# The 1/sqrt of the RMS norms as one power operation on GpSimd in place of seven VectorE operations

## The chip, the cores and the metric

The kernel runs on one core of a Trainium2 chip. The core has a matrix engine (TensorE, in the profile PE, with its weight loads as PEld), three engines for elementwise work (VectorE is DVE, ScalarE is ACT, GpSimd is POOL), and DMA queues that are issued mostly by SyncE (SP). The metric is the device time of one execution in microseconds; lower is better.

## The reference, cut to what matters

A stream of 256 prompt frames and another of 64 sample frames (320 tokens, 1024 features) goes through two layers: a Mamba-2 mixer with a ConvFFN, then, after a shared latent of that stream, multi-head latent attention (MLA) with a ConvFFN. All four sub-layers are wrapped in two norms, x = x + post_norm(f(pre_norm(x))), and the norm is

```
def rmsnorm(x, g):
    xf = x.astype(F32)
    y = xf * lax.rsqrt(jnp.mean(xf * xf, axis=-1, keepdims=True) + EPS)
    return (y * g.astype(F32)).astype(x.dtype)
```

The same function norms the gated output of the Mamba mixer in four groups of 512 features, the MLA latent (256 features) and the query latent (384). What the change touches is the `rsqrt` here and nothing else.

## The kernel before, in words

All activations lie transposed, features on the 128 partitions and the 320 tokens along the row, so that x is eight tiles of 128x320. Every projection is done with weights and activations split into a high and a low part, and three matmuls of a block (high x high, high x low, low x high: `mm3`, L281) stand for one. Weights come in by SP's queue into three buffers `wr`; ScalarE makes the high part `wh` (L326, L329), VectorE the low part `wl` (L328, L330); in MLA GpSimd makes some of the low parts, on the same line L328.

A norm sums over features, that is over partitions. It takes these steps: ScalarE squares the eight tiles and GpSimd or VectorE adds them up (L442); PE multiplies the sum with ones and so gets a column of sums per block of 128 tokens, 128x3 in PSUM (`toksum`, L362); VectorE turns it into the mean square plus epsilon (`mean`, L356, tile `nwv`; or L399, tile `nwl`, at a layer's end); `newton` (L336 to L351) makes 1/sqrt of it by an integer trick for the first guess and two steps of refinement, seven VectorE operations of 128x3, in lines L344 to L350; PE transposes the broadcast columns, which lays the result out over all partitions, 128x320 (`spread`, L369); and the result is used from PSUM or copied by ScalarE first (`rstd_sb`, L388).

There are 13 such norms: at the start of the Mamba input projection and of both up-projections (`outer`, which multiplies the un-normed x in the meantime and scales afterwards); one for each of the four gate groups of the Mamba mixer (`gate_steps`, applied on VectorE in L992); four at the ends of the sub-layers (`late_rstd`, tile `nwl`, where PE runs filler matmuls on a constant tile, L375, before and after the spread; none before the last one); a joint one of MLA with 128x6 columns (tile `rr`, L1110); and the one of the queries (tiles `vq` and `rq`, L1146 and L1147).

The kernel is written in program order, and a scheduler lays the instructions of each engine out anew from its own estimate of their durations. Only at the sub-layer boundaries is the order of VectorE and ScalarE kept as written (`region`). Each engine then runs its list strictly in order. `outer` records the end of the norm as `self.gate`, and the weight splits of the coming tiles are ordered behind that instruction.

Of the kernel before, what the change touches and what calls it, by code (L numbers as in the profile page):

```python
# [9 lines left out]
I32 = mybir.dt.int32  # L10
NOSYNC = mybir.DependencyInfo(mybir.DependencyClass.NoSync, mybir.DependencyReason.DATA)
AF = mybir.ActivationFunctionType
ALU = mybir.AluOpType
# [3 lines left out]
P = 128  # L17
# [32 lines left out]
RSU = 0.7235248917065753  # L50
RS = -0.6537252216689711, 0.8935148218557297, -3.0692990050469557, 2.7565293438350165
# [8 lines left out]
def _vec_layout():  # L60
    if VEC:
        return VEC
    o = 0
    for name, n in (
        ("mix_pre0", 8), ("mix_pre1", 8), ("mix_post0", 8), ("mix_post1", 8),
        ("ffn_pre0", 8), ("ffn_pre1", 8), ("ffn_post0", 8), ("ffn_post1", 8),
        ("kv_in", 8), ("kv_g", 2), ("q_g", 3),
        ("scw", 96), ("scb", 24), ("fcw0", 132), ("fcw1", 132), ("fcb0", 44), ("fcb1", 44),
        ("dtb", 1), ("alog", 1), ("sd", 16), ("sng", 16),
        ("sst", 72), ("fst0", 88), ("fst1", 88),  # L70
    ):
        VEC[name] = (o, n)
        o += n
    VEC["_n"] = (o, 0)
    return VEC
# [10 lines left out]
class Kern:  # L86
# [248 lines left out]

    def newton(self, v, pool, tag):  # L336

        nc = self.nc
        tt, ts, stt = nc.vector.tensor_tensor, nc.vector.tensor_scalar, nc.vector.scalar_tensor_tensor
        n = v.shape[1]  # L340
        r = self.t(pool, [P, n], tag, bufs=2)
        b = self.t(pool, [P, n], f"nwb{n}", bufs=2)
        u = self.t(pool, [P, n], f"nwu{n}", bufs=2)
        ts(r.bitcast(I32), v.bitcast(I32), -0.5, 1597463007.0, op0=ALU.mult, op1=ALU.add)  # L344
        tt(out=b, in0=r, in1=r, op=ALU.mult)
        stt(out=u, in0=b, scalar=RSU, in1=v, op0=ALU.mult, op1=ALU.mult)
        stt(out=b, in0=u, scalar=RS[0], in1=u, op0=ALU.add, op1=ALU.mult)
        stt(out=u, in0=u, scalar=RS[2], in1=u, op0=ALU.add, op1=ALU.mult)
        stt(out=r, in0=b, scalar=RS[1], in1=r, op0=ALU.add, op1=ALU.mult)
        self.nw_end = stt(out=r, in0=u, scalar=RS[3], in1=r, op0=ALU.add, op1=ALU.mult).ins  # L350
        return r  # L351

    def mean(self, src, dim, pool):
# [246 lines left out]
    def run(self):  # L600
        nc, tc, ctx, a = self.nc, self.tc, self.ctx, self.a
        _vec_layout()
        cp = ctx.enter_context(tc.tile_pool(name="cp", bufs=1, reuse_waits="tile"))
        self.wp = ctx.enter_context(tc.tile_pool(name="wp", bufs=1, reuse_waits="tile"))
        self.pst = None
        self.psum(**PSM)
        self.vec = self.t(cp, [P, VEC["_n"][0]], "vec")
        self.con = self.t(cp, [P, CON["cos"][0]], "con")
        self.x = self.t(cp, [P, KD, T], "x")
        self.ones = self.t(cp, [P, P], "ones")  # L610
        self.scratch = self.t(cp, [P, 1], "scratch")
        self.warm = self.t(cp, [P, 256], "warm", mybir.dt.bfloat16)
        self.pe_end = None
        nc.vector.memset(self.warm, 0.0)
        nc.vector.memset(self.ones, 1.0)
        nc.scalar.activation(out=self.scratch, in_=self.ones[:, 0:1], func=AF.Copy)
        self.busy(self.pb(), WARM)
        self.build_stream()
        self.wi = 0
        self.ident = self.c("ident")  # L620
        self.ssm()
        self.ffn(0)
        self.mla()
        self.ffn(1)
        self.residual(a["o_y"])
        self.yst.close()
        self.pst.close()
# [887 lines left out]
```

## Time and profile before

| what | value |
| --- | --- |
| median of 3 runs | 995.41 us (995.04, 995.41, 996.72) |
| the profiled execution | 998.17 us, span 996.4 us, mean granted clock 0.985 |
| PE busy | 959.9 us (96%) |
| VectorE busy | 757.7 us (76%), 1437 instructions |
| ScalarE busy | 605.1 us (61%) |
| GpSimd busy | 350.7 us (35%), 597 instructions |
| DMA | 135.55 MB, 136 GB/s on average |

Rows of the timeline have the start in us from the span's begin, the duration in us, the engine, the line, the operation, output<-inputs, the sizes and the count; in brackets stands how long the engine had been idle before, and what ended that. PE's weight loads (PEld) run ahead of its matmuls. The sub-layers end at about 272 (Mamba), 519 (first ConvFFN), 743 (MLA) and 983 us (second ConvFFN).

### The profile page before, as it was taken

The page shows a single profiled execution, that of the slowest core. Times are in us where ns is not written, and L with a number is a line of the kernel's source. Part 1 is how long each engine was busy: PE and PEld are TensorE (multiplying, and loading weights), DVE is VectorE, ACT ScalarE, POOL GpSimd, SP SyncE. Part 2 cuts the span into 40 slices and gives each one's busy share as a digit, 9 for nine tenths or more (in the row PEclk, how much of TensorE's full clock was granted, in tenths as well). Part 3 has the DMA queues.
Part 4 walks back from the last instruction along what each step waited for, and adds up shares of the span by engine and source line. Part 5 has one row for each costly group of instructions (what it writes and reads, how often), then busy time and mean ns, then how long its engine had stood idle before and what let it go on. Part 6 is the DMA issues. An engine that isn't in the chain of part 4 may idle for free.

```text
span 996.4 us, 18044 instructions
## 1 busy us (share of the span) xinstructions
PE 959.9 (96%) x6585; PEld 929.7 (93%) x6585; DVE 757.7 (76%) x1437; ACT 605.1 (61%) x1201; POOL 350.7 (35%) x597
## 2 busy tenths in 40 slices
PE   7899999999999999999999999999999999999995
PEld 6899999979989999999999899999999999999994
DVE  7879889797488998774547998886538999775433
ACT  6568886734556687664443677774544778665330
POOL 4823231200045665430005765530004767441001
PEclk9999999998999999999999999999999999999998
DMA  7376646442334544455641222133443455445531
GB/s 251 120 212 190 188 138 204 132 154 96 101 94 131 169 149 150 149 186 165 194 125 35 86 70 78 50 102 114 143 136 105 132 167 169 150 143 145 152 115 54
DMA packets 45802, 135.55 MB, mean 136 GB/s; under 512 B 5392, under 2 KB 9616, under 8 KB 45712
## 3 DMA queue, kind: packets, MB, share of 16 engines
q1 hardware_dynamic: 45424, 134.05, 43.1%
q8 instruction: 52, 0.85, 0.4%
q14 instruction: 38, 0.31, 0.1%
q10 hardware_dynamic: 288, 0.33, 0.1%
HBM read 130.25 MB, written 4.11 MB: 135 GB/s over the span
## 4 chain that ended last, share of the span: by engine, by line
PE 79%; DVE 10%; DMA 3%; POOL 3%; issue 3%; ACT 2%; SPq 0%; POOLq 0%; ACTq 0%; DVEq 0%
PE pm L283 46%; PE pm L284 23%; PE px L283 2%; DMA dc<-acd 2%; PE pr L362 1%; PE px L952 1%; DVE wl L328 1%; POOL xacc L442 1%; PE px L284 1%; PE px L943 1%; PE px L935 1%; ACT wh L326 1%; DVE mx L1267 1%; POOL xn L478 1%; DVE y L450 1%
## 5 line engine op out<-in xcount | busy, mean ns | idle before, releaser
L328 DVE TENSOR_TENSOR wl<-wr,wh 128x1024 fp32r<-128x1024 f32 (+2 forms) x204 | 244.8, 1201 | 115.4 <-ACT wh L326 114.6
L326 ACT ACTIVATE wh<-wr 128x1024 fp32r<-128x1024 f32 (+4 forms) x235 | 227.6, 972 | 154.2 <-PE pm L283 126.7
L283 PE MATMUL pm<-xnh,wh 128*128 128x320 f32 x784 | 243.4, 312 | 2.1 <-ACT xnh L329 1.8
L283 PE MATMUL pm<-xnl,wh 128*128 128x320 f32 x784 | 245.0, 313 | 0.3 <-DVE xnl L330 0.3
L284 PE MATMUL pm<-xnh,wl 128*128 128x320 f32 x784 | 243.1, 311 | 0.0
L283 PEld LDWEIGHTS pm<-xnh,wh 128*128 128x128 f32 x784 | 147.6, 189 | 4.8 <-ACT xnh L329 2.0
L283 PEld LDWEIGHTS pm<-xnl,wh 128*128 128x128 f32 x784 | 147.8, 189 | 1.7 <-issue 1.2
L284 PEld LDWEIGHTS pm<-xnh,wl 128*128 128x128 f32 x784 | 147.8, 189 | 1.2 <-issue 1.2
L284 PE MATMUL pm<-ah,wl 128*128 128x320 f32 x452 | 141.0, 313 | 0.0
L283 PE MATMUL pm<-al,wh 128*128 128x320 f32 x452 | 140.4, 311 | 0.0
L283 PE MATMUL pm<-ah,wh 128*128 128x320 f32 x452 | 139.9, 313 | 0.0
L649 DVE SCALAR_TENSOR_TENSOR cv<-ext,vec,cv 128x322 f32<-128x322 f32 x176 | 97.1, 566 | 5.4 <-ACT cv L647 3.0
L643 POOL COPY fsave<-ext 128x2 f32<-128x2 f32 x88 | 72.2, 821 | 53.4 <-ACT ext L640 49.1
L636 POOL MEMSET ext<- 128x2 f32 (+1 forms) x112 | 10.8, 98 | 221.3 <-DVE al L330 66.0
L283 PEld LDWEIGHTS pm<-ah,wh 128*128 128x128 f32 x452 | 85.3, 190 | 1.7 <-ACT ah L329 1.5
L284 PEld LDWEIGHTS pm<-ah,wl 128*128 128x128 f32 x452 | 85.4, 189 | 1.1 <-issue 1.0
L283 PEld LDWEIGHTS pm<-al,wh 128*128 128x128 f32 x452 | 85.5, 189 | 0.0
L328 POOL TENSOR_TENSOR wl<-wr,wh 128x512 fp32r<-128x512 f32 (+2 forms) x31 | 43.7, 1425 | 102.3 <-ACT wh L326 100.9
L283 PE MATMUL pm<-xgl,wh 128*128 128x320 f32 x220 | 68.4, 314 | 1.0 <-DVE xgl L426 1.0
L284 PE MATMUL pm<-xgh,wl 128*128 128x320 f32 x220 | 68.3, 314 | 1.0 <-DVE wl L330 0.7
L283 PE MATMUL pm<-xgh,wh 128*128 128x320 f32 x220 | 62.6, 316 | 4.6 <-ACT xnh L329 2.4
L647 ACT ACTIVATE cv<-ext,vec 128x322 f32<-128x322 f32 x88 | 57.0, 654 | 10.0 <-POOL ext L637 6.8
(396 smaller groups left out, 2138.5 us busy)
## 6 DMA issues: line engine op xcount, KB each, us to landing
wr<-w_up SPq DMA_DIRECT2D x76, 512.0 KB, 3.3
wr<-w_in SPq DMA_DIRECT2D x37, 512.0 KB, 3.8
wr<-w_dn SPq DMA_DIRECT2D x32, 512.0 KB, 3.5
wr<-w_out SPq DMA_DIRECT2D x16, 512.0 KB, 3.6
wr<-w_o SPq DMA_DIRECT2D x16, 512.0 KB, 3.4
wr<-w_up_k SPq DMA_DIRECT2D x16, 384.0 KB, 3.1
wr<-w_dn SPq DMA_DIRECT2D x16, 384.0 KB, 3.2
dc<-acd SPq DMA_DIRECT2D x8, 512.0 KB, 7.0
```

Of the source, the lines that this page charges most:

```text
L283: for i in (mm(out, wh, xh, start=first, stop=False), mm(out, wh, xl, start=False, stop=False), mm(out, wl, xh, start=False, stop=last)):
L284: mm(out, wl, xh, start=False, stop=last)):
L326: self.high_ins = nc.scalar.activation(out=hdst, in_=src, func=AF.Copy).ins
L328: return lambda: e.tensor_tensor(out=ldst, in0=src, in1=hdst.bitcast(F32), op=ALU.subtract)
L362: i = self.nc.tensor.matmul(ps[:, o + b:o + b + 1], acc[:, l0:l0 + 128], self.ones[:, 0:1], start=True, stop=True)
L442: nc.gpsimd.tensor_tensor(out=acc, in0=acc, in1=s, op=ALU.add)
L450: tt(out=yk, in0=yk, in1=r, op=ALU.mult)
L478: nc.gpsimd.tensor_tensor(out=xn, in0=self.x[:, k, :], in1=rstd, op=ALU.mult)
L636: nc.gpsimd.memset(ext[:, 0:m], 0.0)
L643: nc.gpsimd.tensor_copy(out=rows_out[:, 0, :], in_=ext[:, TP:TP + m])
L647: nc.scalar.activation(out=c, in_=ext[:, 0:n], func=AF.Identity, scale=w(0), bias=b)
L649: nc.vector.scalar_tensor_tensor(out=c, in0=ext[:, i:i + n], scalar=w(i), in1=c, op0=ALU.mult, op1=ALU.add)
```

## The change

`newton` becomes one GpSimd operation: the mean square raised to the power of a tile that holds -0.5. That tile, `half`, is 128x8 and set once at the start of the kernel by VectorE. `self.nw_end`, the instruction that `outer` passes on as `self.gate`, is now that GpSimd operation. The two scratch tiles `nwb` and `nwu` are gone. Whole:

```
--- before.py
+++ after.py
@@ -335,19 +335,8 @@
 
     def newton(self, v, pool, tag):
 
-        nc = self.nc
-        tt, ts, stt = nc.vector.tensor_tensor, nc.vector.tensor_scalar, nc.vector.scalar_tensor_tensor
-        n = v.shape[1]
-        r = self.t(pool, [P, n], tag, bufs=2)
-        b = self.t(pool, [P, n], f"nwb{n}", bufs=2)
-        u = self.t(pool, [P, n], f"nwu{n}", bufs=2)
-        ts(r.bitcast(I32), v.bitcast(I32), -0.5, 1597463007.0, op0=ALU.mult, op1=ALU.add)
-        tt(out=b, in0=r, in1=r, op=ALU.mult)
-        stt(out=u, in0=b, scalar=RSU, in1=v, op0=ALU.mult, op1=ALU.mult)
-        stt(out=b, in0=u, scalar=RS[0], in1=u, op0=ALU.add, op1=ALU.mult)
-        stt(out=u, in0=u, scalar=RS[2], in1=u, op0=ALU.add, op1=ALU.mult)
-        stt(out=r, in0=b, scalar=RS[1], in1=r, op0=ALU.add, op1=ALU.mult)
-        self.nw_end = stt(out=r, in0=u, scalar=RS[3], in1=r, op0=ALU.add, op1=ALU.mult).ins
+        r = self.t(pool, [P, v.shape[1]], tag, bufs=2)
+        self.nw_end = self.nc.gpsimd.tensor_tensor(out=r, in0=v, in1=self.half[:, 0:v.shape[1]], op=ALU.pow).ins
         return r
 
     def mean(self, src, dim, pool):
@@ -613,6 +602,8 @@
         self.pe_end = None
         nc.vector.memset(self.warm, 0.0)
         nc.vector.memset(self.ones, 1.0)
+        self.half = self.t(cp, [P, 8], "half")
+        nc.vector.memset(self.half, -0.5)
         nc.scalar.activation(out=self.scratch, in_=self.ones[:, 0:1], func=AF.Copy)
         self.busy(self.pb(), WARM)
         self.build_stream()
```

Over the whole kernel this takes 91 instructions (13 x 7) from VectorE's list, puts one memset there, and adds 13 to GpSimd's. Lines of the changed kernel are 11 lower than those of before from `mean` to `outer`, 9 lower behind the memset. Since the scheduler counts with other engines and durations, it also lays out the list of the other engines anew, most of all in the Mamba stage; the boundaries keep their order.

In the rows that follow, each engine's list stands in the order in which it runs; the numbers behind the names tell tiles apart and differ between the two programs.

First place: GpSimd at the boundary from the first ConvFFN to MLA. `fsave` is the saved end of the convolution, `wl` a low part of MLA's first weights. Before:

```order
L644 COPY fsave_3201<-ext_5379 128x2
L328 TENSOR_TENSOR wl_6334<-wr_6118,wh_6333 128x768
L454 TENSOR_TENSOR x_72<-x_72,y_5408 128x320
L442 TENSOR_TENSOR xacc_6256<-xacc_6256,xsq_6269 128x320
L442 TENSOR_TENSOR xacc_6256<-xacc_6256,xsq_6276 128x320
```

With the change:

```order
L635 COPY fsave_3163<-ext_5325 128x2
L339 TENSOR_TENSOR rk_6176<-nwl_6159,half_78 128x3
L328 TENSOR_TENSOR wl_6272<-wr_6064,wh_6271 128x768
L443 TENSOR_TENSOR x_72<-x_72,y_5354 128x320
L431 TENSOR_TENSOR xacc_6194<-xacc_6194,xsq_6207 128x320
```

The power stands between the last copy and the weight split, so the split runs behind it.

Second place: VectorE in `outer` of the first up-projection, around 302 us. Before:

```order
L328 TENSOR_TENSOR wl_3442<-wr_3391,wh_3441 128x896
L356 TENSOR_SCALAR nwv_3469<-pr_3465 128x3
L344 TENSOR_SCALAR rk_3471<-nwv_3469 128x3
L345 TENSOR_TENSOR nwb_564_3472<-rk_3471 128x3
L346 SCALAR_TENSOR_TENSOR nwu_565_3473<-nwb_564_3472,nwv_3469 128x3
L347 SCALAR_TENSOR_TENSOR nwb_564_3472<-nwu_565_3473 128x3
L348 SCALAR_TENSOR_TENSOR nwu_565_3473<-nwu_565_3473 128x3
L349 SCALAR_TENSOR_TENSOR rk_3471<-nwb_564_3472,rk_3471 128x3
L350 SCALAR_TENSOR_TENSOR rk_3471<-nwu_565_3473,rk_3471 128x3
L330 SCALAR_TENSOR_TENSOR wl_3484<-wr_3415,vec_70,wh_3483 128x128
L328 TENSOR_TENSOR wl_3484<-wr_3415,wh_3483 128x896
```

With the change:

```order
L328 TENSOR_TENSOR wl_3396<-wr_3345,wh_3395 128x896
L345 TENSOR_SCALAR nwv_3423<-pr_3419 128x3
L330 SCALAR_TENSOR_TENSOR wl_3430<-wr_3369,vec_70,wh_3429 128x128
L328 TENSOR_TENSOR wl_3430<-wr_3369,wh_3429 128x896
L330 SCALAR_TENSOR_TENSOR wl_3462<-wr_3393,vec_70,wh_3461 128x128
```

The weight splits, which read two tiles of SBUF, follow the mean at once.

Third place: PE around a gate norm late in the Mamba stage, at about 219 us before (`rk` in the transposes of line 369, now 358; `ah` and `al` are the gated activations of earlier groups, lines 918 to 952 the scan). Before:

```order
L362 MATMUL pr_2357<-ones_73,sz_2135 128x1 x3
L935 MATMUL px_2535<-dc_359_2125,xa_2531 64x128 x8
L943 MATMUL px_2544<-ct_1847,hp_2475 128x128 x4
L952 MATMUL px_2551<-xa_2532,bcs_2428 128x512
L918 MATMUL px_2603<-con_71,xs_1911 64x128
L918 MATMUL px_2603<-con_71,xs_1971 64x128
L918 MATMUL px_2603<-con_71,xs_2029 64x128
L918 MATMUL px_2603<-con_71,xs_2089 64x128
L369 MATMUL pr_2373<-con_71,rk_2363 128x128 x3
L935 MATMUL px_2612<-dc_361_2130,xa_2608 64x64 x8
L943 MATMUL px_2621<-ct_1847,h_387_2318 128x64 x4
L952 MATMUL px_2658<-xa_2609,bcs_2490 128x512
```

With the change:

```order
L284 MATMUL pm_2539<-ah_103,wl_2467 128x320
L283 MATMUL pm_2540<-ah_103,wh_2466 128x320
L283 MATMUL pm_2540<-al_104,wh_2466 128x320
L358 MATMUL pr_2343<-con_71,rk_2341 128x128 x3
L284 MATMUL pm_2540<-ah_103,wl_2467 128x320
L283 MATMUL pm_2541<-ah_103,wh_2466 128x320
L283 MATMUL pm_2541<-al_104,wh_2466 128x320
L284 MATMUL pm_2541<-ah_103,wl_2467 128x320
```

Where the transposes of the norm stood between steps of the scan with no other matmul near, they stand among the matmuls of the output projection; the steps of the scan are spread over that stretch in the same way.

## The prediction

> **What bounds the kernel now.** I read the head of the page first, then the chain that ended last, then the busy time by stretches of the span.
>
> ```profile
> span 996.4 us, 18044 instructions
> PE 959.9 (96%) x6585; PEld 929.7 (93%) x6585; DVE 757.7 (76%) x1437; ACT 605.1 (61%) x1201; POOL 350.7 (35%) x597
> PE 79%; DVE 10%; DMA 3%; POOL 3%; issue 3%; ACT 2%; SPq 0%; POOLq 0%; ACTq 0%; DVEq 0%
> ```
>
> TensorE is busy for 959.9 of 996.4 us, so at most about 36 us is to be had without touching the matmuls. VectorE, from which the change takes work, holds only 10% of the last chain. Two stretches of the Mamba stage (columns: stretch, length, then busy us of PE, PEld, DVE, ACT and POOL, granted clock, DMA share, GB/s) show where VectorE is the fuller engine:
>
> ```profile
> 18.00:50.00 32.00, 26.87 (x169) 26.05 (x170) 28.27 (x66) 16.78 (x28) 23.00 (x27) 0.95 0.36 117
> 200.00:240.00 40.00, 37.64 (x257) 33.20 (x257) 35.67 (x72) 15.16 (x25) 0.24 (x2) 0.91 0.36 123
> ```
>
> In the first, PE is idle for 32.00 - 26.87 = 5.1 us and VectorE for 3.7; in the second PE is idle for 2.4 us and its clock is down to 0.91. So seven small VectorE operations can matter in two ways: as latency, where everything waits for one norm (the layer boundaries), and as room on VectorE (the Mamba stage). The first can be counted from the trace, the second only bounded.
>
> **The price of the power operation, d.** No instruction of this trace raises to a power, so d is unknown and everything is worked out as a function of it. The nearest rows are two-input operations on GpSimd (columns: least/median/largest ns):
>
> ```profile
> L442 POOL TENSOR_TENSOR xacc<-xacc,xsq x28: 877/1008/1629, 7.7 to 763.2; 128x320 f32<-128x320 f32 x28
> L328 POOL TENSOR_TENSOR wl<-wr,wh x31: 1007/1295/2083, 520.7 to 652.6; 128x512 fp32r<-128x512 f32 x15, 128x768 fp32r<-128x768 f32 x8, 128x384 fp32r<-128x384 f32 x8
> ```
>
> The least of 320 columns is 877 ns, and the least of the other row, which I take for its 384 columns, 1007 ns: (1007 - 877)/64 = 2.0 ns a column and 877 - 320 x 2.03 = 227 ns fixed. Three columns of an ordinary operation would be 0.23 us: the lower bound. For the upper one, if a power takes as much work as the seven operations it stands for, it is 7 x 0.23 = 1.6 us. I take d = 0.8 us, between the two and nearer to the plain operation, since most of it is the fixed part. It may also be above 1.6 us: that is a rival below. Where a result crosses from one engine to the next I add 0.1 us each way (VectorE to PE took 985.50 - 985.39 = 0.11 in the rows that follow), so that the new path from the mean square to PE's transposes is 0.2 + d.
>
> The Trainium skill (GPSIMD Engine Reference, section 4.1, Engine selection) says that a two-input elementwise operation is about twice as slow on GpSimd as on VectorE, which speaks against such a move. This trace agrees for 320 columns: 877 ns on GpSimd, 0.49 us for the VectorE sum of line 452 below. By that rule alone, with VectorE's 0.16 us for a three-column operation, d would be an estimated 0.32 us, and the terms below would add up to about 0.5 us more at the end, 0.5 us more at the ConvFFN-to-MLA boundary and nothing elsewhere.
>
> **Boundary by boundary.** The last norm has nothing beside it:
>
> ```profile
> 983.98 0.16 DVE L399 SCALAR_TENSOR_TENSOR nwl<-pr,nwv 128x3 f32<-128x3 f32 x1 [3.94 <-PE pr L362]
> 985.23 0.16 DVE L350 SCALAR_TENSOR_TENSOR rk<-nwu,rk 128x3 f32<-128x3 f32 x1
> 985.50 0.30 PEld L369 LDWEIGHTS pr<-con,rk 128*128 128x128 f32 x3 [1.65 <-issue]
> ```
>
> The mean square is there at 984.14 and PE starts to spread at 985.50: 1.36 us. It becomes 0.2 + 0.8, so the gain is 1.16 - d = **0.36**, all of it on the path, since the output follows.
>
> The boundary from the first ConvFFN to MLA:
>
> ```profile
> 520.10 1.52 PEld L375 LDWEIGHTS <-warm 128*128 128x128 bf16 x14
> 520.39 0.16 DVE L399 SCALAR_TENSOR_TENSOR nwl<-pr,nwv 128x3 f32<-128x3 f32 x1 [2.94 <-PE pr L362]
> 520.70 1.80 POOL L328 TENSOR_TENSOR wl<-wr,wh 128x768 fp32r<-128x768 f32 x1 [77.44 <-ACT wh L326]
> 520.79 1.73 DVE L345 TENSOR_TENSOR nwb<-rk 128x3 f32<-128x3 f32 x1
> 523.49 0.30 PEld L369 LDWEIGHTS pr<-con,rk 128*128 128x128 f32 x3 [1.87 <-issue]
> 524.66 0.49 DVE L452 TENSOR_TENSOR xgh<-x,y 128x320 fp32r<-128x320 f32 x1
> ```
>
> Here one of the seven takes 1.73 instead of 0.16 us: it starts 0.09 us after GpSimd's 1.80 us split and ends 0.02 us after it. In the new order the power stands ahead of that split on GpSimd (first place of the section on the change). So it runs from 520.65 to 520.65 + d, PE can spread at 520.75 + d but not before its filler matmuls end at 520.10 + 1.52 = 521.62, and the split runs from 520.65 + d to 522.45 + d. VectorE's sum into xgh (line 452), for which the next stage waits, reads two SBUF tensors as line 345 did, and would be held until the split ends: 523.25 at d = 0.8 against 524.66, a gain of 2.21 - d = **1.41**. The cost has moved from one victim to the next, which is later.
>
> The boundary from MLA to its ConvFFN, and the one from the Mamba stage to the first ConvFFN:
>
> ```profile
> 744.11 1.52 PEld L375 LDWEIGHTS <-warm 128*128 128x128 bf16 x14
> 744.39 0.16 DVE L399 SCALAR_TENSOR_TENSOR nwl<-px,nwv 128x3 f32<-128x3 f32 x1 [3.06 <-PE px L362]
> 745.86 0.30 PEld L369 LDWEIGHTS px<-con,rk 128*128 128x128 f32 x3 [0.24 <-DVE rk L350]
> ```
>
> ```profile
> 273.23 2.46 PEld L375 LDWEIGHTS <-warm 128*128 128x128 bf16 x14
> 273.52 0.16 DVE L399 SCALAR_TENSOR_TENSOR nwl<-pr,nwv 128x3 f32<-128x3 f32 x1 [1.74 <-PE pr L362]
> 275.76 0.65 PEld L369 LDWEIGHTS pr<-con,rk 128*128 128x128 f32 x3
> ```
>
> At 744 the fillers end at 745.63 and the spread starts at 745.86: the gain is **0.23** as long as 744.55 + 0.2 + d is below 745.63 (d up to 0.88), and 1.11 - d after that. At 273 the fillers run to 275.69 and set the start: **0** for d up to 275.76 - 273.88 = 1.9, since the norm is covered today already.
>
> **Inside the stages.** The norms at the start of a projection (`outer`) and the joint one of MLA (six columns) have matmuls beside them:
>
> ```profile
> 302.77 0.16 DVE L356 TENSOR_SCALAR nwv<-pr 128x3 f32<-128x3 f32 x1 [5.22 <-PE pr L362]
> 304.12 0.35 DVE L330 SCALAR_TENSOR_TENSOR wl<-wr,vec,wh 128x128 fp32r<-128x128 f32 x1
> 304.39 1.08 DVE L328 TENSOR_TENSOR wl<-wr,wh 128x896 fp32r<-128x896 f32 x1
> 305.18 0.39 PEld L369 LDWEIGHTS pr<-con,rk 128*128 128x128 f32 x3
> ```
>
> ```profile
> 19.30 0.16 DVE L356 TENSOR_SCALAR nwv<-pr 128x3 f32<-128x3 f32 x1 [0.25 <-PE pr L362]
> 21.67 0.30 PEld L369 LDWEIGHTS pr<-con,rk 128*128 128x128 f32 x3 [0.79 <-PE pm L284]
> ```
>
> ```profile
> 544.87 0.17 DVE L344 TENSOR_SCALAR rr<-vs 128x6 int32<-128x6 int32 x1
> 546.68 0.39 PEld L369 LDWEIGHTS pr<-con,rr 128*128 128x128 f32 x3
> ```
>
> PE spreads 305.18 - 302.93 = 2.25, 21.67 - 19.46 = 2.21 and 546.68 - 544.87 = 1.81 us after the mean, and in none of the three was the norm the last to arrive. So they count **0** while 0.2 + d stays below these, and the cover that would be gone is 2.0 us (1.6 for the six columns). The third such norm, of the last ConvFFN, is of the same form. The weight splits behind the norm move up on VectorE (second place of the section on the change), which nobody waited for.
>
> The norm of the queries:
>
> ```profile
> 556.22 0.15 DVE L1146 SCALAR_TENSOR_TENSOR vq<-pr,ex 128x3 f32<-128x3 f32 x1
> 557.47 4.15 POOL L1202 TENSOR_TENSOR qs<-q,qs 32x320 fp32r<-32x320 f32 x6 [1.00 <-ACT qs L1196]
> 560.81 0.15 DVE L1148 TENSOR_SCALAR sc<-rq 128x2 f32<-128x2 f32 x1
> ```
>
> ```profile
> PE pm L283 <- DVE qll L328: 1.1, 3, 0.6
> ```
>
> The seven stretch over most of 556.4 to 560.8, partly held by GpSimd's qs. GpSimd is idle for 1.00 us ahead of those, where the power fits for d up to about 1. PE's waits for qll there are 1.1 us in all: gain between 0 and 1.1, and I take half, **0.5**.
>
> **The Mamba stage.** Four gate norms run while VectorE is nearly full:
>
> ```profile
> 217.17 0.15 DVE L344 TENSOR_SCALAR rk<-nwv 128x3 int32<-128x3 int32 x1
> 219.51 0.16 DVE L350 SCALAR_TENSOR_TENSOR rk<-nwu,rk 128x3 f32<-128x3 f32 x1
> 221.97 1.47 DVE L992 TENSOR_TENSOR yg<-yg,pr 128x1280 f32<-128x1280 f32 x1
> ```
>
> The first six of the seven take until about 218.2 and the last waits behind two others. That is some 1.2 us of VectorE for each of five norms (four gates, one `outer`), 6 us in all. The scheduler has also laid the stage out anew: where the scan of the last group had no independent matmul between its steps, dense projection matmuls now stand between (third place of the section on the change), which can fill the 2.4 us of idle PE and the 9% of clock that are lost in 200 to 240 (0.09 x 40 = 3.6 us). Against that, an order that a planner made on its own idea of d can also bring new waits. Bounds: a gain of 2.4 + 3.6 = 6, and a loss of 3, about one such wait at two norms. I take **1.5**, the middle of the two.
>
> **Sum.** 0.36 + 1.41 + 0.23 + 0 + 0 + 0.5 + 1.5 = 4.0 us. The profiled execution took 998.17 us (1.8 around its span of 996.4), so it becomes 994.2. The runs have their median at 995.41, 2.76 below it; taking this off gives **991.4 us**. A measurement of this kernel tells about 0.2%, 2 us, from no change.
>
> **Rivals.** *B, no change that can be measured.* d lies between 1.1 and 1.6 us, or the Mamba stage gives nothing. At d = 1.3 with no gain there: 2.21 - 1.3 = 0.9, 1.11 - 1.3 = -0.2, 1.16 - 1.3 = -0.1, together 0.6 us: 994.8. For it: five of the thirteen norms are covered, and the bound of 1.6 is not far off. Against it: the 1.73 us stall goes in either case.
>
> *C, the power is slow.* It decides from d = 1.6 on, where the three exposed boundaries give 0.6 - 0.5 - 0.4, hence nothing. At d = 3: 273 costs 1.1 (3 - 1.9), 520 costs 0.8, 744 costs 1.9, the end costs 1.8, three outer norms 1.0 each, the query norm some 2, and the joint one, if six columns take twice as long, 6.2 - 1.8 = 4.4: 15.0 us, less the 1.5 of the Mamba stage: 13.5, or 1009. At d = 2, where the outer norms just hold: 0.1 - 0.2 + 0.9 + 0.8 + 0 + 1 + 2.4 = 5.0, less 1.5: 3.5, or 998.9. For it: all GpSimd rows here are sums, differences, products and copies, so nothing excludes it. Against it: it has only three or six columns, and 1.6 us is already seven times the plain operation.
>
> *D, VectorE keeps GpSimd from its operands.* What happened to VectorE at 520 happens the other way round in the Mamba stage:
>
> ```profile
> L643 POOL COPY ssave<-ext x24: 176/663/5697, 26.7 to 176.0; 128x3 f32<-128x3 f32 x24
> 27.64 5.70 POOL L643 COPY ssave<-ext 128x3 f32<-128x3 f32 x1
> 27.81 1.22 DVE L328 TENSOR_TENSOR wl<-wr,wh 128x1024 fp32r<-128x1024 f32 x1
> ```
>
> A copy of three columns that takes 176 ns by itself took 5.70 us while VectorE went from one operation with two SBUF inputs to the next; the median is 663 ns. The Trainium skill (SBUF — State Buffer, section Who interferes with whom) states this as a lock: a VectorE operation with two SBUF inputs and a GpSimd operation that reads SBUF shut each other out. The trace agrees with it in both directions. In the new order VectorE's splits follow the mean at once, so at 302 two pairs of them (0.35 + 1.08 each) could hold the power until 302.93 + 2.86 = 305.8 and PE until 306.7, 1.5 us later than today; the same at 19. If at each of four gates the wait lasts about as long as that copy's and 2 us of it is not covered, this is 3 + 8 against 2.5 for the boundaries and the queries: 8.5 us slower, 1003.9 with nothing from the new layout. It decides from about half a us at each gate on (3 + 2 against 2.5). Against it: it limits itself, since a VectorE that reaches the gate has to wait for the norm and so lets go.
>
> **How the numbers follow.** The forecast (d from 0.3 to 1.1, the new layout of the Mamba stage a small gain) gets 0.49, B 0.20, C 0.18 and D 0.13. The forecast's own range: at best d = 0.3, 0.86 + 1.87 + 0.23 (the spread at 520 cannot start before 521.62, 1.87 earlier), 1.1 for the queries and 4 for the Mamba stage, 8.1 us, 987.3; at worst d = 1.1, 1.2 and nothing more, 994.2. The whole range takes in the lower end and a bit of the 6 us bound, 986.5, and C up to d = 3, 1009. Faster by over 0.2%: 0.49; within: 0.21; slower: 0.30 (C and D).
>
> **What would show it.** Line 339 in the new profile gives d and its spread: 0.3 to 1.1 us for three columns and a largest value under 3 us. At the end, the nwl-to-spread distance falls from 1.36 to about 1.0 us. At 520 the 1.73 us row is gone, and GpSimd's split starts after the power. At 273, 302 and 545 the spread stands where it stood. In the last 40 us of the Mamba stage PE's idle time falls below 2.4 us and the clock rises above 0.91. The forecast is wrong if line 339 has a median above 1.6 us (then C), or if PE or VectorE waits for line 339 at the gates for more than 1 us each (then D).

## The result, and the profile after

The changed kernel takes 987.62 us (median of 6 runs, 985.95 to 989.06) beside 996.72 us for the kernel before (median of 6): ratio 0.9915, 95% interval 0.9899 to 0.9931, or 8.5 us faster; the two medians are 9.1 us apart. The forecast was 991.4 us with a range from 986.5 to 1009.0. The sign was right and the time lies in the range, but the gain is about twice the forecast 4.0 us. Which of its terms were wrong is the matter of what follows. One execution below, the profiled one of the kernel with the power operation in the Mamba stage alone, ran at a granted clock of 0.56 and took 1556.21 us; it enters no ratio, and no number below is from its trace.

The head of the page of the changed kernel:

```profile
span 985.2 us, 17961 instructions
PE 956.4 (97%) x6585; PEld 930.2 (94%) x6585; DVE 744.3 (76%) x1347; ACT 603.7 (61%) x1201; POOL 368.3 (37%) x610
PE 83%; DVE 10%; POOL 2%; issue 2%; ACT 1%; DMA 0%; POOLq 0%; DVEq 0%; ACTq 0%
```

VectorE lost 13.4 us of busy time, and its share of the last chain is 10% as before. PE's share rose from 79% to 83% of a shorter span.

The power operation has line 339 in the changed kernel (least/median/largest ns, then first and last start):

```profile
L339 POOL TENSOR_TENSOR rk<-nwv,half x7: 851/900/1764, 19.6 to 756.0; 128x3 f32<-128x3 f32 x7
L339 POOL TENSOR_TENSOR rk<-nwl,half x4: 848/848/850, 268.2 to 973.9; 128x3 f32<-128x3 f32 x4
L339 POOL TENSOR_TENSOR rr<-vs,half x1: 1332/1332/1332, 534.6 to 534.6; 128x6 f32<-128x6 f32 x1
L339 POOL TENSOR_TENSOR rq<-vq,half x1: 1090/1090/1090, 546.1 to 546.1; 128x3 f32<-128x3 f32 x1
```

At the four sub-layer ends d is 0.85 us for three columns. For the seven norms inside the stages the median is 0.90, and for the queries it is 1.09. The one row of six columns has 1.33, which gives an estimate of (1332 - 848)/3 = 161 ns a column and 365 ns fixed. The forecast took 0.8.

The two stretches of the Mamba stage in the changed kernel, in the columns of the table in the prediction:

```profile
18.00:50.00 32.00, 25.90 (x157) 24.73 (x156) 29.54 (x64) 16.95 (x28) 27.16 (x28) 0.89 0.35 117
200.00:240.00 40.00, 40.00 (x296) 36.99 (x296) 29.60 (x45) 17.57 (x23) 2.79 (x4) 1.00 0.40 132
```

From 200 to 240 us PE is full, at full clock, and does 296 matmuls where it did 257. From 18 to 50 it is a little worse off than before.

The time by stages, in two executions each of both kernels (the second profiles are two of the runs below). A stage runs from one norm's mean square on VectorE to the next, or to PE's spread:

| stage | before | before, again | after | after, again | gain |
| --- | --- | --- | --- | --- | --- |
| start to the first boundary's mean square | 273.52 | 273.15 | 267.92 | 268.18 | 5.3 |
| first boundary, to the mean square of `outer` | 29.25 | 27.50 | 27.66 | 27.80 | 0 to 1.6 |
| first ConvFFN, to the one after it | 213.99 | 213.97 | 212.37 | 212.37 | 1.6 |
| ConvFFN-to-MLA boundary, to the joint norm's spread | 26.29 | 26.30 | 24.75 | 24.75 | 1.5 |
| MLA, to its last mean square | 197.71 | 197.85 | 197.90 | 197.86 | 0 |
| MLA-to-ConvFFN boundary, to the mean square of `outer` | 21.73 | 21.71 | 21.54 | 21.54 | 0.2 |
| second ConvFFN | 217.86 | 217.86 | 217.85 | 217.85 | 0 |
| last mean square to the end | 12.42 | 12.44 | 11.59 | 11.72 | 0.8 |

Without the first boundary the gains add up to 9.4 us, and 6.9 of them lie where no norm is exposed: 5.3 us in the Mamba stage and 1.6 us in the first ConvFFN. The 1.6 us that the first boundary seems to have gained comes and goes in the kernel before itself: its first execution had its filler matmuls there at a lower clock (14 weight loads in 2.46 us), the second at full clock (1.52 us), and then its distance is 27.50. Whether the change makes the lower clock rarer there, two executions each can't say.

### The profile page after: what moved, and what is told of

Read it like the earlier page. It is cut to its first block, busy times and chain, and to the rows that moved or that the text cites. A ratio compares the mean times of both kernels' runs of the same rounds, so it can differ in the third digit from the quotient of the medians.

```text
span 985.2 us, 17961 instructions
## 1 busy us (share of the span) xinstructions
PE 956.4 (97%) x6585; PEld 930.2 (94%) x6585; DVE 744.3 (76%) x1347; ACT 603.7 (61%) x1201; POOL 368.3 (37%) x610
## 4 chain that ended last, share of the span: by engine, by line
PE 83%; DVE 10%; POOL 2%; issue 2%; ACT 1%; DMA 0%; POOLq 0%; DVEq 0%; ACTq 0%
PE pm L283 48%; PE pm L284 24%; PE px L283 2%; DVE wl L328 1%; PE px L943 1%; PE px L926 1%; PE px L284 1%; PE pr L351 1%; POOL xacc L431 1%; PE px L934 1%; DVE xnl L330 1%; DVE cv L640 1%; PE px L909 1%; DVE y L439 1%; DVE x L443 1%
## 5 line engine op out<-in xcount | busy, mean ns | idle before, releaser
L284 PE MATMUL pm<-xnh,wl 128*128 128x320 f32 x784 | 245.8, 314 | 0.0
L339 POOL TENSOR_TENSOR rk<-nwl,half 128x3 f32<-128x3 f32 x4 | 3.4, 848 | 211.7 <-DVE nwl L388 211.7
```

Source lines behind the costliest of these rows:

```text
L284: mm(out, wl, xh, start=False, stop=last)):
```

## The experiments

Three theories for the Mamba stage: **Room** (VectorE, nearly full there, has 35 operations fewer), **Short norm** (the result reaches PE sooner), and **Order** (the scheduler, which counts with another duration of the norm, has laid the stage out anew, and this layout is better, whoever computes the norm). Each kernel's time is given as its ratio to the kernel before on the same chip, with the 95% interval in brackets; it lies within 0.0013 of the ratio of the two medians, and 0.001 is 1.0 us. "PE rows" are the entries of PE's list, in the order in which it runs. The edits are cut to what matters and partly put in words; they are against the changed kernel, but for the order by hand, which is against the kernel before.

**Which norms carry it.** One kernel has the power operation in the five norms of the Mamba stage alone, one in the other eight alone:

```
         c = count of the call
-        power operation
+        if c > 4:  seven VectorE operations    (e1; in e2: if c < 5)
+        else:      power operation
```

> The power operation in the five norms of the Mamba stage (its outer and the four gates), the seven VectorE operations in the other eight norms. The lists of the engines in the Mamba stage are those of the changed kernel, behind it those of the kernel before. In the profiles the changed kernel was 5.6 us ahead of the kernel before at the mean square of the first boundary (267.92 against 273.52). Theory: these 5.6 us come from the Mamba stage itself, and the eight other norms give the rest at their own places. Then this kernel reaches that mean square at about 268, gains nothing at 302, 520 and the end, and its median is 5 to 7 us below the kernel before (the norm-to-spread time at the first boundary falls from 2.2 to 1.4 to 2.0 us if the filler matmuls run at full clock). Rival: the 5.6 us are a slow execution of the kernel before; then the median moves by 2 us or less.

Measured: 0.9948 (0.9931 to 0.9965), 5.2 us.

> The reverse: the seven VectorE operations in the five norms of the Mamba stage, the power operation in the other eight. The Mamba stage has the lists of the kernel before. Theory: the first mean square at about 273, then gains of 1.6 in the first ConvFFN (VectorE has no idle time there from 302 to 350, and loses seven operations), 1.5 at the boundary at 520, 0.2 at 744 and 0.4 to 0.8 at the end: 3.5 to 4.5 us in all. Rival for the ConvFFN: the 1.6 us there follow from the new order of the Mamba stage (weights that arrive at other times); then 2 to 2.5 us in all, and PE still waits for VectorE's ext and xnl there.

Measured: 0.9975 (0.9961 to 0.9988), 2.5 us, less than the 3.5 to 4.5 expected. Its timeline:

```profile
272.28 0.16 DVE L408 SCALAR_TENSOR_TENSOR nwl<-pr,nwv 128x3 f32<-128x3 f32 x1 [1.74 <-PE pr L371]
301.31 0.16 DVE L365 TENSOR_SCALAR nwv<-pr 128x3 f32<-128x3 f32 x1 [5.24 <-PE pr L371]
513.69 0.15 DVE L365 TENSOR_SCALAR nwv<-pr 128x3 f32<-128x3 f32 x1
```

The Mamba stage ends at 272.28, near the kernel before, and the ConvFFN takes 513.69 - 301.31 = 212.38, as in the changed kernel. So the 5 us belong to the Mamba stage's own norms, and the 1.6 us do not depend on them. The two gains add up to 7.7 of the 8.5 us. By its stages the second kernel gains 1.6 us in the first ConvFFN, 1.5 behind it, 0.2 behind MLA and 0.4 at the end; why its ratio shows less than their sum stays open.

**VectorE's work put back.** The power operation gives the result, and the seven operations run beside it for nobody:

```
         self.nw_end = gpsimd.tensor_tensor(out=r, in0=v, in1=half, op=pow)
+        the seven VectorE operations on v, into a tile that nobody reads
```

> The changed kernel, with the seven VectorE operations of each norm put back beside the power operation; their result is read by nobody, so VectorE has all its work of before while the norm itself comes from GpSimd. The scheduler's order of the Mamba stage is near that of the changed kernel (226 of the first 1300 PE rows differ, against 781 from the kernel before). Theory Room (the gain is VectorE's freed time): the 5.6 us of the Mamba stage and the 1.6 us of the ConvFFN are lost, only the boundaries at 520 and the end stay, 2 to 3 us: about 993 to 995. Theory Order (the gain of the Mamba stage comes from the new layout): 4 to 6 us of the Mamba stage stay, the 1.6 us of the ConvFFN are lost: about 989 to 990.

Measured: 0.9946 (0.9929 to 0.9962), 5.4 us. Its end of the Mamba stage, and its last stretch:

```profile
268.60 0.16 DVE L405 SCALAR_TENSOR_TENSOR nwl<-pr,nwv 128x3 f32<-128x3 f32 x1 [1.74 <-PE pr L368]
200.00:240.00 40.00, 40.00 (x296) 37.01 (x295) 33.18 (x57) 18.11 (x25) 0.85 (x1) 1.00 0.41 138
```

With all of VectorE's work of before, in a layout near that of the changed kernel (226 of the first 1300 PE rows differ), the stage keeps 4.7 of its 5.3 us, so Room is not the main thing. The test has a limit: operations that nobody waits for can be put into gaps, which those on the path can't. Most of the 3 us that this kernel loses lies elsewhere: 2.0 in MLA (the query norm's mean square to the last one of MLA is 190.4 in place of 188.4) and 0.7 at the ConvFFN-to-MLA boundary. In the ConvFFN it loses only 0.3 of the 1.6, since there the scheduler spread the seven over the weight splits.

**Norms put back without a new layout.** The seven operations return to the third and fourth gate, and the gates wait for their result; 38 of 1300 PE rows change place:

```
+        if c in (3, 4):  seven VectorE operations
         else:            power operation
```

> The changed kernel, with the seven VectorE operations back at the third and fourth gate norms of the Mamba stage, the power operation at the other eleven. The engines' lists of that stage stay those of the changed kernel but for 38 of 1300 PE rows, so scan and projection remain mixed. Theory Order (the layout carries the gain of the Mamba stage): within 1 us of the changed kernel, 987 to 989, and PE busy 39.5 us or more between 200 and 240 us. Theory Room or shorter norm: two norms of 1.2 to 2.3 us on a full VectorE come back, 1.5 to 3 us over the changed kernel, 989 to 991.

Measured: 0.9926 (0.9907 to 0.9945). The changed kernel gave 0.9915 and 0.9911, so this one is 1.1 to 1.5 us slower, which the intervals don't tell from no difference. The stage ends where it ended:

```profile
208.64 0.14 DVE L365 TENSOR_SCALAR nwv<-pr 128x3 f32<-128x3 f32 x1
267.68 0.16 DVE L408 SCALAR_TENSOR_TENSOR nwl<-pr,nwv 128x3 f32<-128x3 f32 x1 [1.75 <-PE pr L371]
200.00:240.00 40.00, 39.83 (x294) 36.55 (x293) 31.47 (x60) 16.60 (x23) 0.23 (x2) 1.00 0.39 133
```

The gain of the stage lies in this stretch: by the matmuls between 18 and 240 us the changed kernel is 40 ahead (1539 against 1499, quoted further below), and in 200 to 240 alone it is 39 ahead (296 against 257); what the stretches ahead of it gain and lose cancels out. In the second profiles it is 34 and 42. Both norms that fall into this stretch are here computed as before, on VectorE, and PE does 294. So it is the layout that fills it, neither Room nor Short norm.

What the layout takes away can be read from PE's waits between 200 and 240 us. The kernel before has these, both at steps of the scan (where the wait, how long in all, how often, the longest):

```profile
PE px L935 <- DVE xa L925: 1.2, 1, 1.2
PE px L935 <- issue: 1.1, 1, 1.1
```

The changed kernel has none there, and the one with the two norms put back has 0.2 us for another tile. They end at 216.08 and 221.50. Over 220 to 230 us the kernel before is granted a clock of 0.66 and does 47 matmuls, in both of its profiles; the changed kernel has 1.00 and 74. VectorE is busy 9.97 of these 10 us in the kernel before and still 9.16 with the two norms put back, but there PE has other matmuls to do meanwhile. That the waits bring the lower clock is likely by their order in time and not shown.

**The layout of before, with the power operation at the gates.** The seven operations at the first norm alone bring the first 650 PE rows back to those of the kernel before:

```
+        if c == 0:  seven VectorE operations
         else:       power operation
```

> The changed kernel with the seven VectorE operations at the first norm alone. The first 650 PE rows are those of the kernel before, the last 650 near the run with two power operations at the first norm. Theory Order: between 18 and 120 us as the kernel before (PE 26.9 of 32 busy at 18 to 50), then without its heap of 16 PE rows at 210 to 225 us; 988 to 991. Theory Room or shorter norm: four gates have the power operation, four fifths of the gain of the Mamba stage stay, about 988 too, but with VectorE's waits gone between 120 and 240 and no change in 18 to 50.

Measured: 0.9957 (0.9941 to 0.9974), 991.37 us. The stage ends at:

```profile
272.20 0.16 DVE L408 SCALAR_TENSOR_TENSOR nwl<-pr,nwv 128x3 f32<-128x3 f32 x1 [1.75 <-PE pr L371]
131.23 4.92 POOL L343 TENSOR_TENSOR rk<-nwv,half 128x3 f32<-128x3 f32 x1 [1.26 <-DVE nwv L365]
136.20 0.30 PEld L378 LDWEIGHTS pr<-con,rk 128*128 128x128 f32 x3 [2.55 <-POOL rk L343]
```

Only 1.1 us of the gain is left, where Room and Short norm would keep four fifths, 4.2. The time lies 0.4 us above Order's 988 to 991. But this layout also brings something that the changed kernel escapes: the power of the first gate takes 4.92 us, and PE's weight loads wait 2.55 us for it. With that added back it is 3.7 of 4.2, and more if such a wait costs more than it lasts, as it does in the next run. So this run does not part the theories; it shows that the layout decides what the power runs beside.

**Two power operations.**

```
-        r = v ** -0.5
+        q = v ** 0.25; r = q ** -2      (e4: all norms; f3: gates; f1: first norm)
```

> The changed kernel, with two power operations in a row at the four gate norms (0.9 us more each), one at the other nine. Lists as in the changed kernel but for 37 of 1300 PE rows. Theory Order: the gate norms are covered by projection matmuls, so within 1 us of the changed kernel, 987 to 989. Rival, a shorter norm is what helped: 0.9 us for each gate, 3 to 4 us over it, 990.5 to 991.5. It also tells what the doubled power costs in the Mamba stage where it does not change the layout.

Measured: 0.9981 (0.9967 to 0.9995), 993.61 us: outside both expectations. The first gate again:

```profile
124.07 0.85 POOL L342 TENSOR_TENSOR nwq<-nwv,half 128x3 f32<-128x3 f32 x1
124.78 1.81 DVE L877 TENSOR_TENSOR dc<-dtt,dc 128x1024 f32<-128x1024 f32 x2
125.00 6.57 POOL L344 TENSOR_TENSOR rk<-nwq,half 128x3 f32<-128x3 f32 x1
130.79 0.54 DVE L650 SCALAR_TENSOR_TENSOR xs<-ext,vec,xs 128x323 f32<-128x323 f32 x1
131.62 0.90 PE L366 MATMUL pr<-con,rk 128*128 128x128 f32 x3 [3.48 <-POOL rk L344]
```

The first power slips through before VectorE begins a row of operations with two SBUF inputs; the second starts 0.22 us behind the first of them, and does not end until 0.24 us behind the last of them (131.33 to 131.57): 6.57 us in place of 0.85. PE waits 3.48 us, and in the 40 us around it the clock is 0.91 and 246 matmuls are done in place of 288. That is rival D, measured at one gate: from its mean square to that of the second gate it is 58.07 us, in the changed kernel 52.32 and 53.60, so the price is 4.5 to 5.8 us. At the end of the stage 7.0 us are lost (275.07 against some 268.05), 1.0 of them behind the second gate's mean square. At the other three gates PE does not wait for the doubled power (0.85 + 0.85 us, at one of them 1.77 + 0.85), and no more than that 1.0 us can be theirs, where three norms that are 0.9 us longer would cost 2.7. So a longer norm is for the most part covered there, which speaks against Short norm, and a norm that is held up by VectorE, as at the first gate, is not.

> Two power operations in a row in place of one (to the power 0.25, then -2), so the norm takes 0.9 us longer on GpSimd and VectorE is as free as in the changed kernel. With the longer norm the scheduler lays the Mamba stage out more as before (482 of the first 1300 PE rows differ from the kernel before, 835 from the changed kernel). Theory Room: the Mamba stage keeps its 5.6 us, the ConvFFN its 1.6, and the boundaries lose 0.9 us each at 520, 744 and the end: about 990 to 991. Theory Order: most of the 5.6 us go too: about 994 to 996.

Measured: 1.0002 (0.9989 to 1.0016). The median, 996.96 us, lies 1 us above what Order put and 6 above Room, but for another reason, so this run decides nothing on the Mamba stage, whose end at 268.73 is nearly that of the changed kernel. The loss is at the boundaries, where GpSimd's order has put its weight split between the two powers:

```profile
511.58 0.85 POOL L340 TENSOR_TENSOR nwq<-nwl,half 128x3 f32<-128x3 f32 x1 [77.37 <-DVE nwl L391]
512.39 1.80 POOL L328 TENSOR_TENSOR wl<-wr,wh 128x768 fp32r<-128x768 f32 x1
514.16 0.85 POOL L342 TENSOR_TENSOR rk<-nwq,half 128x3 f32<-128x3 f32 x1
515.06 0.30 PEld L361 LDWEIGHTS pr<-con,rk 128*128 128x128 f32 x3 [2.49 <-POOL rk L342]
```

That boundary takes 28.83 us in place of 24.75, MLA 0.9 more, the second ConvFFN with its boundary 1.6 more and the end 0.9 more.

> The changed kernel with two power operations in a row at the first norm alone (the Mamba stage's outer), one at the other twelve. The scheduler then begins the stage as in the run with two everywhere (no difference in the first 650 PE rows), which had PE busy 28.6 us at full clock between 18 and 50 us, where the changed kernel has 24.9 at 0.89; the last part has its own order, with the last group's scan in two heaps of 9 and 5 PE rows. Theory Order: the start gains 2 to 4 us on the changed kernel and the end loses 1 to 2: 985 to 988, though its first norm takes longer. Theory that a shorter norm and a free VectorE make the gain: 0.9 us slower than the changed kernel, 988.5 or more.

Measured: 0.9932 (0.9908 to 0.9956), 988.09 us: the same as the changed kernel within the interval. The start is what the layout promised, and the first gate takes it away again (18 to 50 us, then the gate):

```profile
18.00:50.00 32.00, 28.11 (x190) 27.62 (x191) 29.79 (x66) 19.23 (x32) 28.68 (x31) 1.00 0.36 117
127.64 4.90 POOL L347 TENSOR_TENSOR rk<-nwv,half 128x3 f32<-128x3 f32 x1 [1.27 <-DVE nwv L353]
132.59 0.30 PEld L366 LDWEIGHTS pr<-con,rk 128*128 128x128 f32 x3 [2.58 <-POOL rk L347]
```

190 matmuls at full clock between 18 and 50 us against 157 at 0.89. It begins with a norm that is 1 us longer, and so is a further case of a layout that outweighs the norm. Such a start with a first gate that is not held up may be the faster kernel; no run has it.

**The order by hand.** The kernel before, with its seven operations everywhere; the last group's scan is placed between projection matmuls:

```
-        ('z', 3, 3), ...
+        ('z', 3, 0), ...          no step of the scan written between the last group's z blocks
+        each scan matmul of the last group runs behind the last
+        projection matmul that was written ahead of it
```

> The kernel before, seven VectorE operations at all 13 norms; alone the order is changed: the last group's scan steps on PE are ordered one by one behind matmuls of the output projection (some 25 between two), instead of in a row ahead of it. Theory Order: PE is busy 39 us or more of 200 to 240, its clock there is 1.00, the fillers at the first boundary run at full clock, and the median falls by 3 to 5 us to 991 to 993. If VectorE's freed time or the shorter norm made the gain: no gain, 995 to 998.

Measured: 1.0064 (1.0045 to 1.0083), 6.4 us slower, against Order's 3 to 5 us gain; PE is busy 35.43 us of 200 to 240 at a clock of 0.91, where 39 or more at 1.00 were expected.

```profile
200.00:240.00 40.00, 35.43 (x253) 32.87 (x251) 27.44 (x48) 13.87 (x21) 0.23 (x2) 0.91 0.33 109
252.42 0.16 DVE L356 TENSOR_SCALAR nwv<-pr 128x3 f32<-128x3 f32 x1 [1.57 <-PE pr L362]
```

The last gate's mean square has moved from 238 to 252 us, and the projection waits for what hangs on it. To mix scan and projection is therefore not enough, and this run does not show that the changed kernel's layout with seven VectorE operations would be as fast: no run has that kernel, since the scheduler lays another one out as soon as the early norms change. Order is carried by the two runs in which the layout stayed near that of the changed kernel and the work came back (all of VectorE's work: 4.7 of 5.3 us stay; the two norms of 200 to 240: all stays), and it is shown for that stretch. For the first three norms of the stage it stays open.

**The first ConvFFN.** The seven operations at its `outer` alone:

```
+        if c == 6:  seven VectorE operations
         else:       power operation
```

> The changed kernel, with the seven VectorE operations back in one place, the norm at the start of the first ConvFFN. There they stand ahead of the weight splits on VectorE, which has no idle time for 50 us behind them. Theory: this one norm is the 1.6 us that the first ConvFFN became shorter, so the stage from its mean square to the next goes from 212.4 back to 213.7 to 214.0, and the median is 1.3 to 1.6 us over the changed kernel: about 989. Rival: the stage is shorter for what comes before it (clock, weights that arrived): 212.4 stays, within 0.5 us of the changed kernel.

The ends of the stage in the changed kernel, then in this one:

```profile
295.58 0.16 DVE L345 TENSOR_SCALAR nwv<-pr 128x3 f32<-128x3 f32 x1 [5.10 <-PE pr L351]
507.95 0.15 DVE L345 TENSOR_SCALAR nwv<-pr 128x3 f32<-128x3 f32 x1
```

```profile
293.59 0.16 DVE L365 TENSOR_SCALAR nwv<-pr 128x3 f32<-128x3 f32 x1 [3.70 <-PE pr L371]
507.56 0.15 DVE L365 TENSOR_SCALAR nwv<-pr 128x3 f32<-128x3 f32 x1
```

The stage is 507.56 - 293.59 = 213.97 again, where the changed kernel has 212.37 and the kernel before 213.99 and 213.97. The median, 987.77 us and 0.9927 (0.9907 to 0.9946), doesn't resolve 1.6 us; the stage does. So this one norm is the whole 1.6 us. It is gained in the first 57.2 us from the mean square on. PE does 377 matmuls there in the kernel before and 388 in the changed one (11 of them at 0.147 us are 1.6 us); with this norm put back it does 377 again, and 388 where the power operation is in the later norms alone. PE's waits name 1.0 of the 1.6 us. First the kernel before, then the changed one:

```profile
302.80:360.00 57.20, 56.01 (x377) 55.01 (x377) 55.37 (x117) 39.75 (x76) 37.52 (x74) 1.00 0.45 148
PE pm L283 <- DVE ext L642: 0.9, 3, 0.4
PE pm L283 <- DVE xnl L330: 0.3, 1, 0.3
```

```profile
295.60:352.80 57.20, 57.05 (x388) 56.63 (x388) 54.74 (x109) 38.47 (x73) 42.26 (x74) 1.00 0.45 148
PE pm L283 <- DVE ext L633: 0.2, 1, 0.2
```

**Both kernels once more.**

> The kernel before once more, unaltered, for a second profile. If the stage times are those of the kernel: first boundary at 271 to 274 us, PE 37.6 busy of 200 to 240 at a clock of 0.91, first ConvFFN 213.9 to 214.1. If the Mamba stage of its first profile was a slow execution, 268 to 270.

> The changed kernel once more, unaltered, for a second profile and for times on the same chip as its neighbours. If the stage times are those of the kernel and not of one execution: its mean square at the first boundary again at 266 to 269 us, 200 to 240 with PE full, the stage of the first ConvFFN 212.3 to 212.5, the boundary at 511 to the joint norm 24.6 to 24.8, ratio to the kernel before 0.990 to 0.993.

Measured: the kernel before 996.42 us, the changed one 986.74 us, 0.9911 (0.9892 to 0.9931). The stage times are in the table; all come back within 0.4 us but the first boundary.

## Why the prediction was right or wrong, point by point

The forecast time missed by 3.8 us. That the measured one lies in the range is owed to the range's lower end, which takes in a part of the 6 us bound of the Mamba stage, and not to the sum.

**The price d.** Taken 0.8 us, measured 0.85. The lower bound (0.23) and the upper (1.6) held, and rivals B and C, which began at 1.1 and 1.6, did not come about. That 0.8 came so near is luck: the reason given for it, that most of the power is the fixed part of a plain operation, is not borne out. By the estimate above 0.37 of the 0.85 us are fixed, against 0.23, and a column of the power costs 0.16 us, against 0.002. The estimate of 0.32 us that stands beside the sum was too low.

**The exposed boundaries** were right. At the end the distance from mean square to spread fell by 0.37 us against 0.36:

```profile
973.61 0.16 DVE L388 SCALAR_TENSOR_TENSOR nwl<-pr,nwv 128x3 f32<-128x3 f32 x1 [3.94 <-PE pr L351]
973.86 0.85 POOL L339 TENSOR_TENSOR rk<-nwl,half 128x3 f32<-128x3 f32 x1 [77.37 <-DVE nwl L388]
974.76 0.30 PEld L358 LDWEIGHTS pr<-con,rk 128*128 128x128 f32 x3 [1.27 <-POOL rk L339]
```

From there to the end the changed kernel is another 0.3 to 0.5 us shorter, which was not forecast. VectorE's last operation ends 7.3 us behind the spread in all four profiles, so the difference arises behind it, and its cause stays open. At 744 the gain is 0.2 against 0.23. At the ConvFFN-to-MLA boundary it is 1.5 against 1.41, by the steps of the forecast:

```profile
511.57 0.16 DVE L388 SCALAR_TENSOR_TENSOR nwl<-pr,nwv 128x3 f32<-128x3 f32 x1 [2.94 <-PE pr L351]
511.81 0.85 POOL L339 TENSOR_TENSOR rk<-nwl,half 128x3 f32<-128x3 f32 x1 [77.37 <-DVE nwl L388]
512.63 1.81 POOL L328 TENSOR_TENSOR wl<-wr,wh 128x768 fp32r<-128x768 f32 x1
514.04 0.75 DVE L441 TENSOR_TENSOR xgh<-x,y 128x320 fp32r<-128x320 f32 x1
```

The split runs behind the power, and the sum into xgh is the next victim: it takes 0.75 us in place of 0.49 and ends 0.35 us behind the split. The stall of 1.73 us has shrunk to 0.26.

**The norms in the stages, "0".** Right for the second ConvFFN (0.0) and for MLA; wrong for the first ConvFFN, where 1.6 us came. The step that failed is "the weight splits behind the norm move up on VectorE, which nobody waited for". The prediction looked at who waits for the norm's result, and there the cover held: PE spread 2.4 us after the mean square started in both kernels. But the seven operations (302.97 to 304.19, 1.2 us) stood at the head of a queue of VectorE work that had hardly a gap (busy 55.4 of the 57.2 us from 302.8 on), and PE waited for what stood further back in it. It is their place that costs, more than their amount: with the seven put back for nobody, VectorE runs the same 117 operations in these 57 us, but spread among the splits, and only 0.3 us are lost. The first split of 896 columns starts 1.62 us behind the mean square in the kernel before, 0.35 in the changed one and 0.55 in that run. The second ConvFFN has the same code, but there VectorE soon waits for ScalarE's high part: 0.21 us at 769.01 in the kernel before and 1.27 us at the same place in the changed one (758.44), so the time of the seven turned into waiting. That this is why they cost nothing there is argued from these rows; no run tests it.

**The query norm, 0.5.** Measured 0. PE's waits for qll in the changed kernel, and the first qll on VectorE:

```profile
PE pm L283 <- DVE qll L328: 1.1, 3, 0.6
```

```profile
547.76 0.49 DVE L328 TENSOR_TENSOR qll<-pm,qlh 128x320 fp32r<-128x320 f32 x1 [0.91 <-ACT qlh L326]
```

The waits are the 1.1 us of before. VectorE itself sat idle for 0.91 us until ScalarE's qlh was there, so an emptier VectorE could not help.

**The Mamba stage, 1.5 between -3 and 6.** Measured 5.3. This is the term that was mis-sized most. The two things that the prediction named, room on VectorE and the new layout, were right to name, and the bound held; to take the middle was a choice without ground, since nothing in the profile of before prices a layout that has not run. That VectorE is the fuller engine holds from 18 to 50 us, where nothing was gained, but not from 200 to 240 as a whole: there it is busy 35.67 us and PE 37.64, and in the second profile 32.84 and 36.77. It holds in a part of that stretch, from 220 to 230 (9.97 and 8.76 us). In the stage as a whole VectorE is as busy as before, and PE does 40 matmuls more in the same 222 us. First the kernel before, then the changed one:

```profile
18.00:240.00 222.00, 212.98 (x1499) 198.16 (x1500) 196.07 (x366) 146.23 (x250) 66.45 (x101) 0.98 0.51 159
```

```profile
18.00:240.00 222.00, 215.90 (x1539) 202.32 (x1538) 195.77 (x333) 148.59 (x252) 68.70 (x106) 0.98 0.51 162
```

These two rows alone would fit Room too, which would have used its room up. That it is the layout rests on the runs in which VectorE's work and the two norms came back. The part between 200 and 240 us (idle PE of 2.4 us, clock of 0.91) came back in full, as the prediction had set it out as the upper bound.

**Rival D** was the right mechanism for a neighbour, not for this kernel. In the changed kernel the first gate's power runs from 123.64 to 124.49, and VectorE's long row of operations with two SBUF inputs begins at 124.36, 0.72 us behind its start; the largest of all thirteen is 1.76 us. Nothing in the change provides for this start, so it is luck of the layout. In four of the kernels above the same operation took 4.90 to 6.57 us and PE's weight loads waited 2.5 to 3.7 us. The Trainium skill (SBUF — State Buffer, section Who interferes with whom) has the lock itself; these runs agree and add that GpSimd lost it to one VectorE operation after another, not to one.

## What to carry to other kernels

An operation can be on the path in two ways, by its result and by its place ahead of others in a full queue. Before an edit on an engine is costed at nothing, one has to look for the next gap on that engine, and at who waits there, and not only at who waits for the result. Where a scheduler counts durations, a change of a few tenths of a us in one operation can bring another layout that outweighs it; two kernels that differ in it are told apart only by runs that hold the layout and change the work, or the reverse.

## What the runs showed of the hardware that had not been expected

A power operation of 128x3 on GpSimd takes 0.85 us, and by the one row of six columns an estimated 0.16 us for each further column. One VectorE operation of that size takes 0.16 us, but the power stands for seven: from the last mean square to PE's spread it is 0.99 us in place of 1.36, with two hops between engines. The same operation took up to 6.57 us while VectorE ran nine operations with two SBUF inputs back to back. A wait of PE can cost more than it lasts: one of 3.5 us put the next gate off by 4.5 to 5.8 us, with a clock of 0.91 in the 40 us around it. The clock is no fixed function of the program, though: between 18 and 50 us the kernel before was granted 0.95 in one execution and 1.00 in the other, and the fillers of its first boundary ran at low clock in one and at full clock in the other.
